# FFN output projection: when weight sums, activation rounding and loads are issued in each step

## The chip, the cores and the metric

One core of one Trainium2 chip runs the kernel. The metric is the device time of one execution in microseconds. Before the change the median of three runs is 2488.52 us (2488.05 to 2489.48).

## The reference

The reference is one layer of a streaming encoder: a normalised mixer (sparse attention and a state-space branch), then a normalised SwiGLU feed-forward network. The change lies in the last matrix product of the network, `f`:

```python
    for _ in range(DEPTH):
        ...
        x = x + gate_m * rmsnorm(mix, post_norm_mix)
        h2 = rmsnorm(x, pre_norm_ffn) * (1.0 + scale_f) + shift_f
        u_gate, u_up = jnp.split(h2 @ w_ffn_in, 2, axis=-1)
        f = (jax.nn.silu(u_gate) * u_up) @ w_ffn_out
        x = x + gate_f * rmsnorm(f, post_norm_ffn)
    return x
```

All arrays are float32. The hidden activation has 1024 positions and 2816 columns, `w_ffn_out` is 2816 by 1024.

## The kernel before

**Tiling.** The product is computed as a Strassen-like scheme of seven half-size products, in the order "1567342". Each of them multiplies a 1408 by 512 combination of weights with a 1408 by 512 combination of activations. The combinations of activations are made earlier (`gate_up`) and lie in device memory (`d_a`). The combinations of weights are made on the way: product 5 sums two blocks into a tile `ws` (L1389), product 6 subtracts from it (L1392), product 7 takes a difference of two fresh blocks (L1395), product 3 uses `ws` again (L1398); products 1, 4 and 2 take a block as it is.

**Precision.** Each float32 operand is split into a rounded part and a rest: ScalarE copies it to the reduced type (`whi`, `ah`, L245), and GpSimd (for weights, `wlo`) or VectorE (for activations, `al`) subtracts (L246). A product of two such pairs takes three matmuls (`P3`: rounded weight with rounded activation, rounded weight with the rest, rest of the weight with rounded activation).

**Steps.** The first six products run as 66 steps, 11 row blocks `j` for each product. A step `i` is 12 matmuls of 128x512 on TensorE (four output blocks `m`, three matmuls each, L1418). While it runs, the step also loads, sums and splits for later steps. Product 2, the seventh, comes last: it is computed in two halves of 256 columns with all 11 row blocks of its weights resident (`late_w`, tiles `wfh` and `wfl`), so that the output can be normalised and written while the second half runs.

**What sets the order.** Inside the block `in_order` (L1457 and on) every engine, and the queue of SyncE that issues all loads, works in exactly the order in which the code is written; nothing overtakes. Engines wait for each other through semaphores alone. A load waits until the tile that it overwrites is free. The buffers that matter are:

- the raw weights (`wraw`): 4 tiles, shared with `gate_up`'s weights;
- the rounded weights and their rests (`whi`, `wlo`): 3 tiles each, so the weights for step `i + 2` can be written once step `i - 1` has been multiplied;
- `EV`: 9 tiles for raw activations (`al`, as loaded), the second block of product 7 (`wt`) and sums of squares;
- `H_` (32) and `Q` (26): the split activations of one product each in turn, the `ws` tiles and the resident weights.

A name can stand for two tiles: `al` is a raw activation as loaded and also the rest that is made from it.

In a step before the change VectorE and ScalarE first make the weights of step `i + 2` (sum, then `whi`), and then the activations of the next product (`ah`, then `al`); between them VectorE or ScalarE takes the result of the product that has ended out of PSUM (`evict`, four times for each product). In product 4's steps the block also loads and splits one row block of the resident weights for each step.

Of the kernel before, what the change touches and what calls it, by code (L numbers as in the profile page):

```python
# [11 lines left out]
F32R = mybir.dt.float32r  # L12
BF = mybir.dt.bfloat16
AF = mybir.ActivationFunctionType
OP = mybir.AluOpType
# [25 lines left out]
PRODUCT = {n: i for i, n in enumerate("1567342")}  # L41
# [26 lines left out]
def build(tc, a, dbg=None, stop=99, slots=None):  # L68
# [9 lines left out]
    H_ = Arena(ctx, tc, "H", n_slots["H"], 512)  # L78
# [13 lines left out]
    def f(x):  # L92
        return x.bitcast(F32)
# [39 lines left out]
    class Stream:  # L133
# [13 lines left out]
        def load(self):  # L147
            src, kt = self.q[len(self.tiles)]
            raw, hi, lo = self.tile(0, F32), self.tile(1, F32R), self.tile(2, F32R)
            behind(SP.dma_start(raw[:, :kt], src))  # L150
            behind(S.activation(hi[:, :kt], raw[:, :kt], AF.Copy))  # L151
            behind(G.tensor_tensor(lo[:, :kt], raw[:, :kt], f(hi[:, :kt]), op=OP.subtract))  # L152
            self.tiles.append((hi, lo))
# [90 lines left out]
    def split_to(src, hi, lo, lo_eng=None):  # L244
        S.activation(hi, src, AF.Copy)  # L245
        (lo_eng or V).tensor_tensor(lo, src, f(hi), op=OP.subtract)  # L246

    def split(alloc, src, name, shape=None, lo_eng=None):
        hi = alloc(name + "h", shape, F32R)
        lo = alloc(name + "l", shape, F32R)  # L250
        split_to(src, hi, lo, lo_eng)
        return hi, lo
# [14 lines left out]
    def rspread(r, nt=4):  # L267
        pt = bank("prn")
        for t in range(nt):
            T.transpose(pt[:, t * P:(t + 1) * P], r[:, t:t + 1].to_broadcast([P, P]), ident)  # L270
        return pt
# [1093 lines left out]
    def flat(t):  # L1365
        return t.rearrange("p m n -> p (m n)")
# [4 lines left out]
    def out_load(name, j):  # L1371

        def load(k, m, to=None):
            r = flat(W.tile(0, F32)) if to is None else to
            SP.dma_start(r, a["w_ffn_out"][k][:, 512 * m:512 * m + 512])
            return r

        k1, k2 = 2 * j, 2 * j + 1
        if name == "5":
            S_[j] = load(k1, 1, place(j)("ws"))  # L1380
            return load(k2, 1)
        if name == "7":
            return load(k1, 0), load(k1, 1, EV("wt"))
        return load(*{"1": (k1, 0), "6": (k1, 0), "3": (k2, 0), "4": (k2, 1), "2": (k2, 0)}[name])

    def out_weights(name, j, raw, alloc=None, lo_eng=G):
        if name == "5":
            w = S_[j]
            V.tensor_tensor(w, w, raw, op=OP.add)  # L1389
        elif name == "6":  # L1390
            w = S_[j]
            V.tensor_tensor(w, w, raw, op=OP.subtract)  # L1392
        elif name == "7":
            w = raw[0]
            V.tensor_tensor(w, w, raw[1], op=OP.subtract)  # L1395
        elif name == "3":
            w = S_.pop(j)
            V.tensor_tensor(w, raw, w, op=OP.subtract)  # L1398
        else:
            w = raw  # L1400
        if alloc is None:
            hi, lo = (flat(W.tile(x, F32R)) for x in (1, 2))
        else:
            hi, lo = alloc("wfh", dt=F32R), alloc("wfl", dt=F32R)
        split_to(w, hi, lo, lo_eng=lo_eng)
        return hi, lo

    def act_load(name, j):
        r = EV("al")
        SP.dma_start(r, d_a[PRODUCT[name], j])  # L1410
        return r

    def act_split(name, r):
        return split((H_, Q)[PRODUCT[name] % 2], r, "a")

    def out_mm(o, w, x, m, cl, j):
        for k, (wi, xi) in enumerate(P3):
            T.matmul(o, w[wi][:, P * m:P * m + P], x[xi][:, cl], start=j == 0 and k == 0, stop=j == NP - 1 and k == 2)  # L1418

    def quarter(m):  # L1420
        return [y[:, half(b)] for y in (acc_[m], acc_[4 + m]) for b in BS]
# [14 lines left out]
    def squared(y, cn, sacc):  # L1436
        sq = EV("sqm")[:, 0:cn]
        S.activation(sq, y, AF.Square)
        if sacc is not None:
            V.tensor_tensor(sq, sq, sacc, op=OP.add)  # L1440
        return sq
# [15 lines left out]
    with in_order(mybir.EngineType.PE, mybir.EngineType.Activation, mybir.EngineType.DVE,  # L1457
                  mybir.EngineType.Pool, mybir.EngineType.SP):
        steps = [(n, j) for n in ORDER[:-1] for j in range(NP)]
        raws, ws, xs, late_w = {}, {}, {}, []  # L1460

        def raw_ahead(i):
            if i < len(steps):
                raws[steps[i]] = out_load(*steps[i])

        def weights_ahead(i):
            if i < len(steps):
                ws[steps[i]] = out_weights(*steps[i], raws.pop(steps[i]))

        raw_ahead(0)  # L1470
        raw_ahead(1)
        for j in range(NP):
            xs["1", j] = act_split("1", act_load("1", j))
            if j < 2:
                weights_ahead(j)
                raw_ahead(j + 2)
        before, banks, s1, prf = None, None, None, None
        for i, (name, j) in enumerate(steps):
            n = ORDER.index(name)
            nxt = ORDER[n + 1]  # L1480
            r = act_load(nxt, j)
            raw_ahead(i + 4)
            late = out_load("2", j) if name == "4" else None
            if j == 0:
                if banks:
                    before = steps[i - 1][0], banks
                banks = [(bank_d if n % 2 and m < 3 else bank)("pfo") for m in range(4)]
            x, w = xs.pop((name, j)), ws.pop((name, j))
            for m in range(4):
                out_mm(banks[m], w, x, m, ALL, j)  # L1490
            if before and j < 4:
                evict(before[0], j, before[1][j])
            weights_ahead(i + 2)
            xs[nxt, j] = act_split(nxt, r)
            if late is not None:
                late_w.append(out_weights("2", j, late, H_ if j < 5 else Q, G if j % 2 else V))
            if name == "3" and 1 <= j < 9:
                c11, c12, c21, c22 = quarter((j - 1) // 2)
                if j % 2:
                    V.tensor_tensor(c12, c12, c22, op=OP.add)  # L1500
                else:
                    V.tensor_tensor(c22, c22, c21, op=OP.add)
                    s1 = squared(c22, 512, s1)
            if name == "4":
                if 1 <= j < 5:
                    s1 = squared(quarter(j - 1)[1], 512, s1)
                if j == 7:
                    r1 = rstd([s1], D)
                if j == 9:
                    prf = rspread(r1)  # L1510
        last, s0, before = banks, None, None
        x1_load(512, 512, 0, 1, 2, 3)
        for c in BS:
            cl, sacc = slice(256 * c, 256 * c + 256), None
            for m in range(4):
                p = bank("pfl")[:, 0:256]
                for j in range(NP):
                    out_mm(p, late_w[j], xs["2", j], m, cl, j)
                if c == 0:
                    evict("4", m, last[m])  # L1520
                    s0 = squared(quarter(m)[2], 512, s0)
                    if m < 2:
                        x1_load(512, 512, 2 * m + 4, 2 * m + 5)
                    else:
                        x1_load(0, 256, 2 * m - 4, 2 * m - 3)
                elif m < 2:
                    x1_load(0, 256, 2 * m + 4, 2 * m + 5)
                V.tensor_tensor(acc_[m][:, cl], acc_[m][:, cl], p, op=OP.add)
                sacc = squared(acc_[m][:, cl], 256, s0[:, 256:512] if c and m == 0 else sacc)
                if c == 0:  # L1530
                    output(2 * m, 512, 512, prf, False)
                    output(2 * m + 1, 512, 512, prf, False)
                elif m == 0:
                    r0 = rstd([before, s0[:, 0:256]], D, nt=2)
                elif m == 1:
                    prf = rspread(r0, 2)
                if c and m > 0:
                    for t in ((0, 1, 2, 3), (4, 5, 6, 7), ())[m - 1]:
                        output(t, 0, 256, prf, False)
                    x1_load(256, 256, *((0, 1, 2, 3), (4, 5, 6, 7), ())[m - 1])  # L1540
            before = sacc
        prf = rspread(rstd([before], D, nt=2), 2)
        for t in range(8):
            output(t, 256, 256, prf, True)
# [78 lines left out]
```

## Time and profile before

| what | value |
|---|---|
| median of three runs | 2488.52 us |
| the profiled execution's own time | 2489.43 us |
| span of the profile, first to last instruction | 2487.6 us |
| TensorE busy | 2377.9 us, 96% of the span |
| VectorE, ScalarE, GpSimd busy | 1599.2, 1245.6, 1036.2 us |
| mean granted TensorE clock | 0.987 |
| the steps of the six products | from 2213.4 to about 2441.25 us |

A row of a timeline gives the start and the duration in us, the engine (PE is TensorE, DVE is VectorE, ACT is ScalarE, POOL is GpSimd, SPq is the queue of SyncE that issues loads), the line of the kernel, the operation and its tiles, and in brackets how long the engine sat idle before it and on whom it waited. A row of the stretches gives the time from and to, its length, and for each engine the busy time with the number of instructions. Matmuls overlap each other, so a busy time of TensorE close to the length does not mean that it runs at its best rate; the distance between the first matmuls of two steps does.

### The profile page before, as it was taken

Reading aid. Unit: us, or ns where it says so; the run is one execution under the profiler, and the core shown is the slowest. Engines: PE = TensorE matmul, PEld = TensorE weight load, DVE = VectorE, ACT = ScalarE, POOL = GpSimd, SP = SyncE. Lnnn points to the kernel's source line nnn. Section 1 sums busy time; section 2 is a strip of 40 time slices with the busy share of each in tenths; the row PEclk is TensorE's granted clock in tenths of the full one; section 3 lists DMA queues with packets and bytes.
Section 4 is the critical chain, followed back from the end, with each engine's and each line's share of the span. In section 5 each row is a group of like instructions: output and inputs, shape, how many; then the busy total and the mean of one; then the engine's idle time right before and its main releaser. Section 6 shows DMA issues by size and latency. Waiting matters only on the chain. (4 is left out here: it accounts for less than half of the span.)

```text
span 2487.6 us, 35107 instructions
## 1 busy us (share of the span) xinstructions
PE 2377.9 (96%) x11878; PEld 1910.2 (77%) x11878; DVE 1599.2 (64%) x3115; ACT 1245.6 (50%) x2350; POOL 1036.2 (42%) x848
## 2 busy tenths in 40 slices
PE   7999999999899999999999999998999999999887
PEld 5888888887678787777776777877877888877656
DVE  4467775798855667765557685445376877456665
ACT  3456665567365664455666565533443223344342
POOL 1321112222443335422335346566576555544334
PEclk9999999999999999999999999999999999999999
DMA  7123123423322334213669885654555555256645
GB/s 265 62 88 123 64 68 95 144 93 112 104 90 87 98 98 132 77 35 107 216 217 301 262 246 170 203 174 128 177 189 172 182 177 170 93 193 209 203 136 186
DMA packets 227652, 369.85 MB, mean 149 GB/s; under 512 B 22624, under 2 KB 84752, under 8 KB 227472
## 3 DMA queue, kind: packets, MB, share of 16 engines
q1 hardware_dynamic: 226752, 367.03, 45.8%
q8 instruction: 94, 1.54, 0.3%
q14 instruction: 86, 0.70, 0.1%
q10 hardware_dynamic: 720, 0.58, 0.1%
HBM read 275.74 MB, written 94.92 MB: 149 GB/s over the span
## 5 line engine op out<-in xcount | busy, mean ns | idle before, releaser
L152 POOL TENSOR_TENSOR wlo<-wraw,whi 128x512 fp32r<-128x512 f32 x242 | 330.0, 1366 | 596.7 <-ACT whi L151 540.0
L1254 PE MATMUL p<-xh,wr 128*128 128x512 f32 x880 | 276.3, 392 | 5.9 <-DVE g L1304 4.3
L151 ACT ACTIVATE whi<-wraw 128x512 fp32r<-128x512 f32 x242 | 151.7, 629 | 229.7 <-issue 67.4
L1248 POOL TENSOR_TENSOR wr<-a,wr 128x512 fp32r<-128x512 f32 x110 | 156.9, 1434 | 124.7 <-ACT wr L1247 99.5
L1254 PEld LDWEIGHTS p<-xh,wr 128*128 128x128 f32 x880 | 166.4, 189 | 41.9 <-DVE g L1304 4.7
L1254 PE MATMUL p<-xl,wr 128*128 128x512 f32 x440 | 172.2, 391 | 0.0
L778 ACT ACTIVATE lg<-lg,mx 128x256 f32<-128x256 f32 (+7 forms) x128 | 98.7, 773 | 95.2 <-DVE mx L775 93.1
L246 DVE TENSOR_TENSOR al<-al,ah 128x512 fp32r<-128x512 f32 x77 | 92.5, 1207 | 78.6 <-ACT ah L245 78.2
L1247 ACT ACTIVATE wr<-a 128x512 fp32r<-128x512 f32 x110 | 68.6, 631 | 143.0 <-PE p L1254 116.7
L1418 PE MATMUL pfo<-ah,wlo 128*128 128x512 f32 x264 | 108.9, 412 | 20.0 <-POOL wlo L246 19.9
L1254 PE MATMUL p<-h2h,wr 128*128 128x512 f32 x352 | 111.9, 394 | 0.0
L1418 PE MATMUL pfo<-ah,whi 128*128 128x512 f32 x264 | 105.7, 400 | 3.9 <-ACT whi L245 3.6
L638 ACT ACTIVATE junk<-acc,cand__2182 128x1024 bf16<-128x1024 f32 (+2 forms) x96 | 86.4, 900 | 45.7 <-DVE cand__2182 L681 28.7
L225 PE MATMUL pos<-yh,wlo 128*128 128x512 f32 x256 | 101.1, 396 | 2.7 <-POOL wlo L152 2.7
L1418 PE MATMUL pfo<-al,whi 128*128 128x512 f32 x264 | 103.6, 392 | 0.0
L225 PE MATMUL pos<-yh,whi 128*128 128x512 f32 x256 | 100.9, 395 | 2.4 <-ACT yh L1120 1.4
L589 DVE SCALAR_TENSOR_TENSOR acc<-rel,widx,acc 128x384 f32<-128x384 f32 (+2 forms) x90 | 87.1, 988 | 24.7 <-ACT rel L584 24.5
L799 PE MATMUL pt<-ident,lg 128*128 128x128 f32 x576 | 90.1, 279 | 12.4 <-ACT lg L778 11.2
L584 ACT ACTIVATE rel<-prel 128x512 f32<-128x512 f32 (+3 forms) x160 | 77.3, 524 | 48.0 <-PE prel L583 44.4
L225 PE MATMUL pos<-yw,whi 128*128 128x512 f32 x256 | 100.3, 392 | 0.0
L1254 PEld LDWEIGHTS p<-xl,wr 128*128 128x128 f32 x440 | 83.2, 189 | 17.3
L904 DVE SCALAR_TENSOR_TENSOR cv<-pw,vec,cv 128x511 f32<-128x511 f32 (+2 forms) x96 | 71.3, 743 | 34.6 <-ACT cv L901 34.5
(580 smaller groups left out, 7189.4 us busy)
## 6 DMA issues: line engine op xcount, KB each, us to landing
wraw<-w_in SPq DMA_DIRECT2D x130, 256.0 KB, 2.9
a<-w_ffn_in SPq DMA_DIRECT2D x120, 256.0 KB, 3.3
wraw<-w_ffn_out SPq DMA_DIRECT2D x77, 256.0 KB, 3.1
al<-d_a SPq DMA_DIRECT2D x77, 256.0 KB, 3.6
adaw<-ada_w SPq DMA_DIRECT2D x64, 256.0 KB, 3.0
al<-d_ac SPq DMA_DIRECT2D x32, 512.0 KB, 5.4
wraw<-w_o_ssd SPq DMA_DIRECT2D x64, 256.0 KB, 3.0
d_a<-kept SPq DMA_DIRECT2D x33, 256.0 KB, 3.3
```

The source lines that it names most:

```text
L151: behind(S.activation(hi[:, :kt], raw[:, :kt], AF.Copy))
L152: behind(G.tensor_tensor(lo[:, :kt], raw[:, :kt], f(hi[:, :kt]), op=OP.subtract))
L225: T.matmul(o, wt[:, k0 + i, :], xs[k][xi][b][:, sl], start=pi == 0 and i == 0 and wt is hi and xi == 0, stop=pi == len(pcs) - 1 and i == l ...
L246: (lo_eng or V).tensor_tensor(lo, src, f(hi), op=OP.subtract)
L584: S.activation(rel[:, 512 * b:512 * b + w_], pr[:, 0:w_], AF.Relu)
L589: V.scalar_tensor_tensor(acc[i][:, 0:n], rel[:, 0:n], ws, acc[i][:, 0:n], op0=OP.mult, op1=OP.add)
L638: S.activation(jk, y, AF.Sign, scale=-1.0, bias=a_, accum_out=o)
L778: S.activation(lg[:, 0:n], lg[:, 0:n], AF.Exp, scale=-1.0, bias=m, accum_out=mx[:, 3:4])
L799: T.transpose(ptv[:, hh, t, :], PR[hh, t][:, j * P:(j + 1) * P], ident)
L1248: G.tensor_tensor(w[:, 1], src, f(w[:, 0]), op=OP.subtract)
L1254: T.matmul(p, w[:, wi, i], X[x][i][xi], start=start and i == 0 and k == 0, stop=i == 3 and k == 2, skip_group_check=True)
L1418: T.matmul(o, w[wi][:, P * m:P * m + P], x[xi][:, cl], start=j == 0 and k == 0, stop=j == NP - 1 and k == 2)
```

## The change

Inside the 66 steps four things move.

1. The sum of the weights is a function of its own (`out_sum`) and is made for step `i + 3`, ahead of everything else that the step does on VectorE. Rounding and splitting the weights (`out_weights`) stays at step `i + 2`.
2. ScalarE rounds the activations (`ah`) first in a step, and `whi` after it. The raw activations are loaded one step earlier (`al_ahead(i + 1)`). VectorE's `al` now comes behind the eviction.
3. Raw weights are loaded five steps ahead where it was four; four of them are issued ahead of the first activations.
4. The resident weights of product 2 are loaded into `EV` tiles (`late_load`), not into the raw weights' tiles, two steps ahead of their split, and are spread over steps 48 to 65, that is over products 3 and 4. GpSimd makes all eleven rests; before, VectorE made six of them.

Besides, the sums of squares in product 4 run in its steps 4 to 7 where they ran in 1 to 4, `rstd` stands at its step 8 where it stood at 7, and the spread of its result over the partitions (`rspread`) follows the first group of product 2.

```diff
-    def out_weights(name, j, raw, alloc=None, lo_eng=G):
+    def out_sum(name, j, raw):
         if name == "5":
             w = S_[j]
             V.tensor_tensor(w, w, raw, op=OP.add)
...
         else:
             w = raw
-        if alloc is None:
-            hi, lo = (flat(W.tile(x, F32R)) for x in (1, 2))
-        else:
-            hi, lo = alloc("wfh", dt=F32R), alloc("wfl", dt=F32R)
-        split_to(w, hi, lo, lo_eng=lo_eng)
+        return w
+
+    def out_weights(w):
+        hi, lo = (flat(W.tile(x, F32R)) for x in (1, 2))
+        split_to(w, hi, lo, lo_eng=G)
         return hi, lo
+
+    def late_load(j):
+        r = EV("late")
+        SP.dma_start(r, a["w_ffn_out"][2 * j + 1][:, 0:512])
+        return r
+
+    def late_split(j, r):
+        return split(H_ if j < 5 else Q, r, "wf", lo_eng=G)
...
-        raws, ws, xs, late_w = {}, {}, {}, []
+        late_at = {4 * NP + 4 + (5 * j + 1) // 3: j for j in range(NP)}
+        raws, ws, xs, als, late_r, late_w = {}, {}, {}, {}, {}, []
...
-        raw_ahead(0)
-        raw_ahead(1)
+        for i in range(4):
+            raw_ahead(i)
         for j in range(NP):
-            xs["1", j] = act_split("1", act_load("1", j))
+            r = act_load("1", j)
             if j < 2:
-                weights_ahead(j)
-                raw_ahead(j + 2)
-        before, banks, s1, prf = None, None, None, None
+                ws[j] = out_weights(raws.pop(j))
+            xs["1", j] = act_split("1", r)
+        raw_ahead(4)
+        al_ahead(0)
...
-            r = act_load(nxt, j)
-            raw_ahead(i + 4)
-            late = out_load("2", j) if name == "4" else None
+            al_ahead(i + 1)
+            raw_ahead(i + 5)
+            if i + 2 in late_at:
+                late_r[i + 2] = late_load(late_at[i + 2])
...
             for m in range(4):
                 out_mm(banks[m], w, x, m, ALL, j)
+            sum_ahead(i + 3)
+            r = als.pop(i)
+            hi, lo = (alloc("a" + k, None, F32R) for k in "hl" for alloc in [(H_, Q)[PRODUCT[nxt] % 2]])
+            S.activation(hi, r, AF.Copy)
+            if i + 2 < len(steps):
+                ws[i + 2] = out_weights(raws.pop(i + 2))
             if before and j < 4:
                 evict(before[0], j, before[1][j])
-            weights_ahead(i + 2)
-            xs[nxt, j] = act_split(nxt, r)
-            if late is not None:
-                late_w.append(out_weights("2", j, late, H_ if j < 5 else Q, G if j % 2 else V))
+            V.tensor_tensor(lo, r, f(hi), op=OP.subtract)
+            xs[nxt, j] = hi, lo
+            if i in late_at:
+                late_w.append(late_split(late_at[i], late_r.pop(i)))
...
             if name == "4":
-                if 1 <= j < 5:
-                    s1 = squared(quarter(j - 1)[1], 512, s1)
-                if j == 7:
+                if 4 <= j < 8:
+                    s1 = squared(quarter(j - 4)[1], 512, s1)
+                if j == 8:
                     r1 = rstd([s1], D)
-                if j == 9:
-                    prf = rspread(r1)
...
+                if c == m == 0:
+                    prf = rspread(r1)
```

**Sums and rounding, in the middle of the steps.** These are ScalarE's instructions around the end of product 6, before the change. The numbers tell the tiles apart; VectorE's sum for `ws_20759` and its rest from `ah_21130` stand beside each other in VectorE's own order.

```order
L245 ACTIVATE whi_21101<-ws_20733 128x512
L245 ACTIVATE ah_21105<-al_21084 128x512
L245 ACTIVATE whi_21126<-ws_20759 128x512
L245 ACTIVATE ah_21130<-al_21109 128x512
L1426 ACTIVATE acc4_20473<-pfo_20843 128x512
```

```order
L1392 TENSOR_TENSOR ws_20733<-ws_20733,wraw_21036 128x512
L246 TENSOR_TENSOR al_21106<-al_21084,ah_21105 128x512
L1392 TENSOR_TENSOR ws_20759<-ws_20759,wraw_21061 128x512
L246 TENSOR_TENSOR al_21131<-al_21109,ah_21130 128x512
L1392 TENSOR_TENSOR ws_20785<-ws_20785,wraw_21086 128x512
```

The same place after the change, ScalarE and then VectorE:

```order
L1510 ACTIVATE ah_21106<-al_21064 128x512
L245 ACTIVATE whi_21109<-ws_20713 128x512
L1510 ACTIVATE ah_21131<-al_21089 128x512
L245 ACTIVATE whi_21134<-ws_20739 128x512
L1510 ACTIVATE ah_21160<-al_21114 128x512
```

```order
L1392 TENSOR_TENSOR ws_20739<-ws_20739,wraw_21041 128x512
L1515 TENSOR_TENSOR al_21107<-al_21064,ah_21106 128x512
L1392 TENSOR_TENSOR ws_20765<-ws_20765,wraw_21066 128x512
L1515 TENSOR_TENSOR al_21132<-al_21089,ah_21131 128x512
L1392 TENSOR_TENSOR ws_20792<-ws_20792,wraw_21091 128x512
```

Before, the rounding `whi_21126` needs the sum `ws_20759` that VectorE does just ahead of it, `ah_21130` stands behind that rounding on ScalarE, and VectorE's `al_21131` needs `ah_21130`; the next sum stands behind `al_21131`. After the change `ah_21106` stands ahead of the rounding, and the rounding behind it (`whi_21109`) takes the sum of the step before (`ws_20713`).

**Loads at the start.** The queue of SyncE around the first steps; lines with a minus stand there before, lines with a plus after the change. L1375 loads raw weights, L1410 (L1418 after) raw activations, and L1324 to L1342 write `gate_up`'s results.

```order
 L1324 DMA d_a<-g_20108 128x512
+L1375 DMA wraw<-w_ffn_out 128x512
 L1326 DMA d_a<-kept 128x512
 L1328 DMA d_a<-kept 128x512
+L1375 DMA wraw<-w_ffn_out 128x512
 L1340 DMA d_a<-p_20069 128x512
 L1342 DMA d_a<-u_20126 128x512
 L1336 DMA d_a<-p_20212 128x512
 L1338 DMA d_a<-kept 128x512
-L1410 DMA al<-d_a 128x512
-L1375 DMA wraw<-w_ffn_out 128x512
-L1410 DMA al<-d_a 128x512
```

The third and fourth raw weights are issued ahead of `gate_up`'s stores and of the first activations.

**Rests of the resident weights.** GpSimd's order in products 3 and 4, before the change:

```order
L246 TENSOR_TENSOR wlo<-ws,whi 128x512 x11
L246 TENSOR_TENSOR wlo<-wraw,whi 128x512 x4
L246 TENSOR_TENSOR wfl<-wraw,wfh 128x512
L246 TENSOR_TENSOR wlo<-wraw,whi 128x512 x2
L246 TENSOR_TENSOR wfl<-wraw,wfh 128x512
```

and after it:

```order
L246 TENSOR_TENSOR wlo<-ws,whi 128x512 x7
L246 TENSOR_TENSOR wfl<-late,wfh 128x512
L246 TENSOR_TENSOR wlo<-ws,whi 128x512 x2
L246 TENSOR_TENSOR wfl<-late,wfh 128x512
L246 TENSOR_TENSOR wlo<-ws,whi 128x512
L246 TENSOR_TENSOR wfl<-late,wfh 128x512
```

GpSimd's first resident rest comes eight weights earlier, in product 3, and there are eleven of them where there were five.

More of the change, by code (lines that the diff above doesn't have):

```diff
@@ L1383, in out_load @@
             return load(k1, 0), load(k1, 1, EV("wt"))
-        return load(*{"1": (k1, 0), "6": (k1, 0), "3": (k2, 0), "4": (k2, 1), "2": (k2, 0)}[name])
-    def out_weights(name, j, raw, alloc=None, lo_eng=G):
+        return load(*{"1": (k1, 0), "6": (k1, 0), "3": (k2, 0), "4": (k2, 1)}[name])
+    def out_sum(name, j, raw):
         if name == "5":
@@ L1459, in build, with sum_ahead, al_ahead @@
         steps = [(n, j) for n in ORDER[:-1] for j in range(NP)]
-        raws, ws, xs, late_w = {}, {}, {}, []
+        late_at = {4 * NP + 4 + (5 * j + 1) // 3: j for j in range(NP)}
+        raws, ws, xs, als, late_r, late_w = {}, {}, {}, {}, {}, []
         def raw_ahead(i):
             if i < len(steps):
-                raws[steps[i]] = out_load(*steps[i])
-        def weights_ahead(i):
+                raws[i] = out_load(*steps[i])
+        def sum_ahead(i):
             if i < len(steps):
-                ws[steps[i]] = out_weights(*steps[i], raws.pop(steps[i]))
-        raw_ahead(0)
-        raw_ahead(1)
+                raws[i] = out_sum(*steps[i], raws[i])
+        def al_ahead(i):
+            if i < len(steps):
+                als[i] = act_load(ORDER[i // NP + 1], steps[i][1])
+        for i in range(4):
+            raw_ahead(i)
         for j in range(NP):
-            xs["1", j] = act_split("1", act_load("1", j))
+            r = act_load("1", j)
             if j < 2:
-                weights_ahead(j)
-                raw_ahead(j + 2)
-        before, banks, s1, prf = None, None, None, None
+                ws[j] = out_weights(raws.pop(j))
+            xs["1", j] = act_split("1", r)
+        raw_ahead(4)
+        al_ahead(0)
+        before, banks, s1 = None, None, None
         for i, (name, j) in enumerate(steps):
@@ L1487, in build @@
                 banks = [(bank_d if n % 2 and m < 3 else bank)("pfo") for m in range(4)]
-            x, w = xs.pop((name, j)), ws.pop((name, j))
+            x, w = xs.pop((name, j)), ws.pop(i)
             for m in range(4):
                 out_mm(banks[m], w, x, m, ALL, j)
+            sum_ahead(i + 3)
[4 more added lines that the diff above has]
+                ws[i + 2] = out_weights(raws.pop(i + 2))
             if before and j < 4:
                 evict(before[0], j, before[1][j])
-            weights_ahead(i + 2)
-            xs[nxt, j] = act_split(nxt, r)
-            if late is not None:
-                late_w.append(out_weights("2", j, late, H_ if j < 5 else Q, G if j % 2 else V))
+            V.tensor_tensor(lo, r, f(hi), op=OP.subtract)
+            xs[nxt, j] = hi, lo
+            if i in late_at:
+                late_w.append(late_split(late_at[i], late_r.pop(i)))
             if name == "3" and 1 <= j < 9:
```

## The prediction

> **What bounds the kernel now.** I read the page's groups first, then the stretches of the six products, then TensorE's timeline inside them, and the waits last. The stage from 2213.4 to 2441.25 us is the one that the change touches. Its busy rows, for the matmuls of the steps and the evictions alone:
>
> ```profile
> 2213.40:2248.10 34.70, 30.68 (x133) 24.63 (x133) 0.00 (x0) 0.55 (x1) 1.00 0.91 294
> 2248.10:2280.40 32.30, 31.33 (x134) 24.41 (x133) 0.00 (x0) 1.77 (x4) 1.00 0.68 215
> 2280.40:2316.30 35.90, 33.16 (x134) 23.89 (x132) 0.00 (x0) 2.32 (x4) 1.00 0.62 190
> 2316.30:2354.50 38.20, 33.95 (x133) 23.61 (x132) 2.70 (x4) 0.00 (x0) 1.00 0.61 197
> 2354.50:2400.10 45.60, 36.49 (x133) 24.53 (x133) 2.70 (x4) 0.00 (x0) 0.96 0.38 129
> 2400.10:2441.25 41.15, 33.56 (x133) 23.59 (x131) 2.71 (x4) 0.00 (x0) 1.00 0.61 194
> ```
>
> The stretches are products 1, 5, 6, 7, 3 and 4, each from its first matmul to the next product's first (132 matmuls; a row counts one or two over the edge). After the length come TensorE, weight loads, VectorE, ScalarE, then clock, DMA share and GB/s. The same work takes 32.3 to 45.6 us, so something other than TensorE sets it. What TensorE can do is seen where it waits for nothing, at the first matmuls of steps 6 and 7:
>
> ```profile
> 2234.48 0.39 PE L1418 MATMUL pfo<-ah,whi 128*128 128x512 f32 x1
> 2237.20 0.39 PE L1418 MATMUL pfo<-ah,whi 128*128 128x512 f32 x1
> ```
>
> A step at TensorE's rate is 2.72 us, a product 11 x 2.72 = 29.92 us. Product 1's stretch also holds 12 matmuls of `gate_up`, so it could take 32.64. Against that the products lose 2.1, 2.4, 6.0, 8.3, 15.7 and 11.2 us: **45.7 us** in all, all that can be won here. The page says whom TensorE waits for:
>
> ```profile
> L1418 PE MATMUL pfo<-ah,wlo 128*128 128x512 f32 x264 | 108.9, 412 | 20.0 <-POOL wlo L246 19.9
> ```
>
> It is the weights' rest, GpSimd's last link. But GpSimd is not full; its own wait leads back through ScalarE to VectorE. One turn in product 6, in order of time:
>
> ```profile
> 2294.71 0.68 DVE L1392 TENSOR_TENSOR ws<-ws,wraw 128x512 f32<-128x512 f32 x1
> 2295.50 0.63 ACT L245 ACTIVATE whi<-ws 128x512 fp32r<-128x512 f32 x1 [1.62 <-DVE ws L1392]
> 2296.04 0.62 ACT L245 ACTIVATE ah<-al 128x512 fp32r<-128x512 f32 x1
> 2296.22 1.29 POOL L246 TENSOR_TENSOR wlo<-ws,whi 128x512 fp32r<-128x512 f32 x1 [1.97 <-ACT whi L245]
> 2296.69 1.36 DVE L246 TENSOR_TENSOR al<-al,ah 128x512 fp32r<-128x512 f32 x1 [1.30 <-ACT ah L245]
> 2297.97 0.68 DVE L1392 TENSOR_TENSOR ws<-ws,wraw 128x512 f32<-128x512 f32 x1
> ```
>
> This is a **ring**: sum, rounding of the weight, rounding of the activation behind it, the activation's rest, and only then the next sum. Its turn is 2297.97 - 2294.71 = 3.26 us, more than 2.72, so it sets the pace. The `al` takes 1.36 us, not 0.69, since it starts in the middle of GpSimd's `wlo` and ends 0.54 us after that (2297.51 to 2298.05): the two do not run at once. Two more rows show both halves of this:
>
> ```profile
> 2400.93 3.44 POOL L246 TENSOR_TENSOR wlo<-wraw,whi 128x512 fp32r<-128x512 f32 x2
> 2401.44 1.78 DVE L246 TENSOR_TENSOR al<-al,ah 128x512 fp32r<-128x512 f32 x1
> 2403.14 0.67 DVE L1432 TENSOR_TENSOR acc<-acc,pfo 128x512 f32<-128x512 f32 x1
> 2403.74 1.18 DVE L246 TENSOR_TENSOR al<-al,ah 128x512 fp32r<-128x512 f32 x1
> ```
>
> Around GpSimd's work up to 2404.37, two `al` are stretched, while the eviction between them, which reads PSUM, keeps its 0.67 us. So only operations with both inputs in SBUF share something with GpSimd. In product 3 the ring holds still more:
>
> ```profile
> 2379.54 0.68 DVE L1502 TENSOR_TENSOR acc<-acc 128x512 f32<-128x512 f32 x1
> 2380.92 0.69 DVE L1440 TENSOR_TENSOR sqm<-sqm 128x512 f32<-128x512 f32 x1 [0.70 <-ACT sqm L1438]
> 2381.53 0.69 DVE L1398 TENSOR_TENSOR ws<-wraw,ws 128x512 f32<-128x512 f32 x1
> ```
>
> The combining of results, and a square that VectorE waits for, stand between `al` and the sum, each 0.6 us or more a turn.
>
> Product 4 has no sums; there ScalarE, and all behind it, wait for the resident weights' load:
>
> ```profile
> ACT wfh L245 <- DMA wraw<-w_ffn_out: 18.8, 9, 3.3
> SPq L1375 <- POOL wlo L246: 11.9, 10, 4.9
> ```
>
> The second row is the load queue, waiting for one of the four raw tiles.
>
> **The change part by part.**
>
> *The sum one step earlier and `ah` first* cut the ring. The rounding then uses a sum of the step before, and `ah` depends on nothing made in this step. What limits a step now is each engine's own work: ScalarE two roundings of about 0.54 from start to start (2295.50 to 2296.04), 1.1 us; VectorE two operations at 0.6 (2380.92 to 2381.53), 1.2, plus 0.6 where it evicts; and what VectorE and GpSimd may not do at once, 1.29 + 0.6 + 0.6 = 2.49 us. All are under 2.72. So products 5, 6 and 7 should run at TensorE's rate: 2.4 + 6.0 + 8.3 = 16.7 us removed. In the four evicting steps of product 7, if evictions did count, 3.09 us stand against 2.72; the seven other steps win back 7 x 0.23 = 1.6, as much as the 4 x 0.37 = 1.5 lost. I leave 1 us for the three products: **15.7 gained**, bounds 10 (the tail of a late load in each) and 16.7.
>
> *The resident weights.* Their loads leave the raw tiles for `EV`, so product 4's wait on `wraw` goes; what replaces it is work. For the shared part I add, at 1.29 for GpSimd and 0.6 for VectorE: product 3 has 11 `wlo` and 4 resident rests (19.4), 11 `al`, 8 sums, 8 combinings and 3 additions of squares (30 x 0.6 = 18.0), in all 37.4 against 29.9. Product 4 has 9 `wlo` and 7 resident rests (20.6), 11 `al` and 4 additions (9.0): 29.6 against 29.9. Product 3 thus falls 7.5 us behind, and step by step the lag still grows to about 10 at steps 61 to 63, where a resident rest, a square, an `al` and a `wlo` come together (3.8 us a step), before the last `wlo` are done and it shrinks. Not all of a lag reaches TensorE: product 5 before lost only 2.4 us though 11 turns at 3.26 are 5.9 over the rate, so the pairs of weights made ahead cover 3.5. I take 10 - 3.5 = 6.5, with 0.5 for `rstd` of the squares, whose last square stands one step ahead of it where it stood three: **7 us lost** of the 26.9 that products 3 and 4 lose now, 19.9 gained. Bounds: 3, if late work of VectorE need not be done in time (activations' rests are wanted a product later), and 13, if evictions cannot use the gaps either (8 x 0.6) and the 1.45 us `pow` of GpSimd is on the path.
>
> The row that speaks against part of this is the price of the six rests that move from VectorE to GpSimd:
>
> ```profile
> L246 DVE TENSOR_TENSOR wfl<-wraw,wfh 128x512 fp32r<-128x512 f32 x6 | 4.7, 785 | 7.6 <-ACT wfh L245 7.6
> L246 POOL TENSOR_TENSOR wfl<-wraw,wfh 128x512 fp32r<-128x512 f32 x5 | 6.8, 1351 | 7.2 <-ACT wfh L245 7.2
> ```
>
> Six times 1.29 for 0.6 is 4.1 us more of the shared time, and it is in the 37.4 and 29.6 above. The Trainium skill, "Perfetto Trace Analysis", section "Optimizing Scalar/DVE Operations", warns that VectorE and GpSimd share a read port of SBUF, so that moving work between the two might not help. By that rule alone this edit would give nothing back; the trace agrees with the port (the stretched `al`), and the sum already holds the loss.
>
> *The start.* Product 1's loss is one stall:
>
> ```profile
> 2206.35 9.51 SPq L1410 DMA_DIRECT2D al<-d_a  x8
> 2220.61 0.64 ACT L245 ACTIVATE ah<-al 128x512 fp32r<-128x512 f32 x1 [1.74 <-DMA al<-d_a]
> 2221.15 0.62 ACT L245 ACTIVATE whi<-wraw 128x512 fp32r<-128x512 f32 x1
> 2221.85 2.02 POOL L246 TENSOR_TENSOR wlo<-wraw,whi 128x512 fp32r<-128x512 f32 x1 [9.39 <-ACT whi L245]
> ```
>
> The third step's rounding stands behind eleven `ah`, and their loads wait for `EV` tiles (9.51 us for eight). After the change one more `ah` stands ahead of that rounding, but the first weight's is done before and two raw loads have left the queue's way: 0.4 + 0.5 us sooner for the loads, 0.5 later for the extra `ah`. The first `al` are also less in GpSimd's way. I take a loss of 1 instead of 2.1: **1.1 gained**, bounds -2.7 (a whole step later, if the extra `ah` waits for a load that is issued after the eleventh) and 2.1.
>
> *Loads five ahead* cost no engine time. Each load of a step without a sum waits for the `wlo` one step nearer than before, so the distance from free tile to use stays four steps. The `rspread` is four transposes of TensorE at either place; I count its move as nothing.
>
> **Sum:** 15.7 + 19.9 + 1.1 = 36.7 us. The profiled execution took 2489.43 (span 2487.6 and 1.83 around it), 0.9 above the median of the runs. 2489.4 - 36.7 = 2452.7; its counterpart as a median is 2451.8. I say **2453**, a little up since the unknowns mostly add stalls.
>
> **The rivals.**
>
> *The shared time takes the ring's place everywhere* (VectorE blocked in its order by GpSimd, so that evictions wait too). For it: the 2.49 of 2.72 leaves 0.23 a step. Against it: 0.67 for an eviction inside GpSimd's work. Products 5 to 7 then lose 4 and products 3 and 4 the upper 13, the start 1: 18 us remain, 27.7 gained, **2461**.
>
> *Loads take its place.* Chain: `wlo` frees a raw tile, the queue issues weights and activations (0.4 + 0.4), the load lands, then `ah`, `whi`, `wlo` (0.5, 0.7, 1.3), three steps ahead of use: a step is a third of the landing time + 3.3. Landing times in the busiest stretch, 2220 to 2262 us:
>
> ```profile
> al<-d_a SPq DMA_DIRECT2D x17, 256.0 KB, 4.3
> wraw<-w_ffn_out SPq DMA_DIRECT2D x16, 256.0 KB, 3.9
> d_a<-u SPq DMA_DIRECT2D x1, 256.0 KB, 5.6
> ```
>
> At 4.3 a step is 2.5, hidden; from 4.9 on it shows. At 5.6 it is 2.97: 0.25 over 33 steps (products 1, 7 and 4) is 8 more than my remaining 9, so 28.7 gained, **2460**. Products 5 and 7 ask for 768 KB in 2.72 us, 289 GB/s, close to the 294 of the first stretch, where DMA was 0.91 busy.
>
> *Slower.* The same chain with `ah` ahead of `whi`: if faster steps push the landing to 10 us, a step is 4.4, 1.7 over in 33 steps = 56, with the 9 that remain 65 against 45.7: about 19 slower, **2508**. It decides against the change from a landing of about 8.2 us on; nothing in the trace is above 5.6.
>
> *The change does not do what it says:* the ring closes over another link (a tile that both sides wait for), the step stays at 3.26 and the time at **2488**. The two orders show no such link.
>
> **How the numbers follow.** Forecast 0.70 (2444 to 2457), shared time 0.12, loads 0.08, another ring 0.04, slower 0.06. The floor is 2488.5 - 45.7, about 2443. The range takes in the bounds of products 3 and 4 and of the start and most of both milder rivals: 2445 to 2471. About 0.2% is what a measurement of this kernel can tell from no change. Faster 0.91, same 0.03, slower 0.06.
>
> **What would show it.** In products 5, 6 and 7 the first matmuls of steps should stand 2.72 us apart and ScalarE's `whi` should wait for TensorE (a free tile), not for VectorE's sum. In product 4 the wait on the load of resident weights should be gone. Products 3 and 4 together should take 62 to 73 us where they took 86.75. Wrong would be: steps of 3 us or more in product 6, `ah` waiting for DMA in most steps, or TensorE waiting long at `rstd`.

## The result, and the profile after

The changed kernel takes 2450.26 us (median of four runs, 2449.83 to 2451.43) against 2488.82 us of the kernel before, run beside it: a ratio of 0.9846, 95% interval 0.9829 to 0.9863, or 38.6 us less. The prediction said 2453 us.

The stretches of products 1, 5, 6, 7, 3 and 4 after the change, columns as in the prediction (from and to, length, busy time and number of instructions of TensorE, weight loads, VectorE and ScalarE, clock, DMA share, GB/s):

```profile
2213.33:2247.05 33.72, 30.54 (x132) 24.63 (x132) 0.00 (x0) 0.00 (x0) 1.00 0.87 285
2247.05:2276.97 29.92, 29.92 (x133) 24.78 (x132) 0.00 (x0) 2.32 (x4) 1.00 0.90 309
2276.97:2306.89 29.92, 29.92 (x133) 24.78 (x132) 0.69 (x1) 2.32 (x4) 1.00 0.60 191
2306.89:2336.81 29.92, 29.92 (x133) 24.78 (x132) 2.73 (x4) 0.00 (x0) 1.00 0.87 289
2336.81:2367.99 31.18, 30.46 (x134) 24.44 (x132) 2.02 (x3) 0.00 (x0) 1.00 0.53 173
2367.99:2401.48 33.49, 30.91 (x132) 24.46 (x132) 3.39 (x5) 0.00 (x0) 1.00 0.69 229
```

Products 5, 6 and 7 now take 29.92 us, which is 11 steps at TensorE's rate of 2.72. The six stretches sum to 188.15 us where they took 227.97 with the same boundaries (first matmul of the steps to the first of product 2): 39.8 us less. From there to the end it is 46.6 us, and was 46.2. All of the gain lies in the stage that was changed. TensorE's wait for the weights' rest, 20.0 us on the page before, is nearly gone:

```profile
L1426 PE MATMUL pfo<-ah,wlo 128*128 128x512 f32 x264 | 103.2, 391 | 2.1 <-POOL wlo L246 2.1
```

One step of product 6, in order of time:

```profile
2290.35 0.68 DVE L1392 TENSOR_TENSOR ws<-ws,wraw 128x512 f32<-128x512 f32 x1
2290.59 0.63 ACT L245 ACTIVATE whi<-ws 128x512 fp32r<-128x512 f32 x1 [1.57 <-POOL wlo L246]
2291.13 0.61 ACT L1510 ACTIVATE ah<-al 128x512 fp32r<-128x512 f32 x1
2291.30 1.29 POOL L246 TENSOR_TENSOR wlo<-ws,whi 128x512 fp32r<-128x512 f32 x1 [1.43 <-ACT whi L245]
2291.78 1.37 DVE L1515 TENSOR_TENSOR al<-al,ah 128x512 fp32r<-128x512 f32 x1 [0.75 <-ACT ah L1510]
2293.07 0.68 DVE L1392 TENSOR_TENSOR ws<-ws,wraw 128x512 f32<-128x512 f32 x1
```

The rounding `whi` at 2290.59 starts while the sum at 2290.35 still runs, so it uses an earlier sum. It starts at the first matmul of its step (2290.57); what held it is the weight tile that TensorE gives back there. The row names GpSimd, whose `wlo` had ended 0.7 us before: a wait for several engines is put down to one. `al` still takes 1.37 us in GpSimd's shadow, but from one sum to the next it is 2293.07 - 2290.35 = 2.72 us.

What is left in the stage above 2.72 us a step is 1.0 us at step 2, 3.1 in steps 53 to 56, and 1.65 at step 63.

### The profile page after: what moved, and what is told of

Read it like the earlier page. It is cut to its first block, busy times and chain, and to the rows that moved or that the text cites. A ratio compares the mean times of both kernels' runs of the same rounds, so it can differ in the third digit from the quotient of the medians.

```text
span 2448.1 us, 35113 instructions
## 1 busy us (share of the span) xinstructions
PE 2360.6 (96%) x11878; PEld 1915.1 (78%) x11878; DVE 1598.2 (65%) x3109; ACT 1242.6 (51%) x2350; POOL 1052.2 (43%) x854
## 5 line engine op out<-in xcount | busy, mean ns | idle before, releaser
L1426 PE MATMUL pfo<-ah,wlo 128*128 128x512 f32 x264 | 103.2, 391 | 2.1 <-POOL wlo L246 2.1
L1515 DVE TENSOR_TENSOR al<-al,ah 128x512 fp32r<-128x512 f32 x66 | 74.6, 1132 | 33.0 <-ACT ah L1510 32.7
```

The costliest lines, as they stand in the source:

```text
L1515: V.tensor_tensor(lo, r, f(hi), op=OP.subtract)
```

## The experiments

All are edits of the changed kernel. The stage's length (first matmul of the steps to product 2) is compared across runs, since the part of the kernel ahead of it differs by several us from execution to execution (it ends between 2208.3 and 2217.6 us in the profiles of this document). Each stage is that of one profiled execution; the changed kernel has 188.15 and, run again, 188.56. The ratio is to the kernel before on the same chip.

### Which half of the order cuts the ring

First, ScalarE makes the weight's rounding ahead of the activation's again; the sum stays a step early.

```diff
-            S.activation(hi, r, AF.Copy)
             if i + 2 < len(steps):
                 ws[i + 2] = out_weights(raws.pop(i + 2))
+            S.activation(hi, r, AF.Copy)
```

> One half of the ring's cut is undone: ScalarE makes the weight's rounding first again and the activation's rounding behind it; the sum stays one step early. Ring theory (either half alone cuts the ring, since the rounding then uses a sum of the step before): products 5, 6 and 7 stay at 2.72 us a step, 2450 to 2453 us. Rival A (the rounding of activations first is what matters): the step goes back to about 3.26, products 5 to 7 lose some 16 us and product 3 more, 2466 to 2480. Rival B (the loads further ahead bring the gain, the order nothing): 2450.

Ratio 0.9848 (0.9834 to 0.9863), median 2454.2 us. Products 5 to 7 take 29.92 us each, stage 190.87. Product 1 loses nothing here, but products 3 and 4 take 68.5 us, 3.8 more than in the changed kernel: the place of the activation's rounding counts there, though not for the ring. Then the other half: the sum for step `i + 2` again, the activation's rounding still first.

```diff
-            sum_ahead(i + 3)
+            sum_ahead(i + 2)
```

> The other half is undone: the sum is made for step i + 2 again, ahead of its rounding in the same step; the activation's rounding stays first. Ring theory: the activation's rest no longer waits for the weight's rounding, so no ring; 2.72 us a step in products 5 to 7, 2450 to 2456 us (some cushion is lost in product 3, where the sum stands behind VectorE's lag). Rival A' (the early sum is what matters): 3.26 a step, 2466 to 2480. Rival B (loads): 2450.

Ratio 0.9832 (0.9816 to 0.9849), 2451.26 us; products 5 to 7 at 29.92 again, stage 189.09. Then both undone, with the eviction ahead as it was; all loads and the resident weights stay as changed.

```diff
-            sum_ahead(i + 3)
...
-            S.activation(hi, r, AF.Copy)
-            if i + 2 < len(steps):
-                ws[i + 2] = out_weights(raws.pop(i + 2))
             if before and j < 4:
                 evict(before[0], j, before[1][j])
+            sum_ahead(i + 2)
+            if i + 2 < len(steps):
+                ws[i + 2] = out_weights(raws.pop(i + 2))
+            r = als.pop(i)
...
+            S.activation(hi, r, AF.Copy)
```

> Both halves are undone: eviction, sum for i + 2, weight's rounding, activation's rounding, activation's rest, in the order of the kernel before; the loads five and one ahead and the spread resident weights stay as changed. Ring theory: steps of 3.26 us in products 5 to 7 and of 3.85 and more in product 3 return; some 16 us there, 12 or more in product 3; 2478 to 2486 us. Rival B (loads bring the gain): 2450 to 2453.

Ratio 0.9975 (0.9962 to 0.9988), 2483.67 us. Products 5, 6, 7 and 3 of this kernel:

```profile
2241.31:2273.55 32.24, 31.22 (x133) 24.39 (x132) 0.00 (x0) 1.78 (x4) 1.00 0.65 215
2273.55:2309.48 35.93, 33.13 (x133) 23.92 (x132) 0.00 (x0) 2.32 (x4) 1.00 0.60 190
2309.48:2347.74 38.26, 34.03 (x133) 23.62 (x132) 2.70 (x4) 0.00 (x0) 1.00 0.58 196
2347.74:2396.52 48.78, 37.45 (x134) 25.39 (x132) 2.70 (x4) 0.00 (x0) 0.93 0.44 148
```

32.24, 35.93 and 38.26 us are, within 0.04, the 32.28, 35.94 and 38.24 of the kernel before. The ring is the cause of what products 5 to 7 lost, either half alone opens it, and the loads alone leave it closed. Products 3 and 4 take 84.7 us together here, 2.2 less than before the change: the new tiles and the spread bring little without the new order.

### The resident weights

They go back to product 4's steps, to the raw weights' tiles, and to both engines; the order of the steps stays as changed.

```diff
-        r = EV("late")
+        r = flat(W.tile(0, F32))
...
-        return split(H_ if j < 5 else Q, r, "wf", lo_eng=G)
+        return split(H_ if j < 5 else Q, r, "wf", lo_eng=G if j % 2 else V)
...
-            if i + 2 in late_at:
-                late_r[i + 2] = late_load(late_at[i + 2])
+            if name == "4":
+                late_r[i] = late_load(j)
...
-            if i in late_at:
-                late_w.append(late_split(late_at[i], late_r.pop(i)))
+            if name == "4":
+                late_w.append(late_split(j, late_r.pop(i)))
```

> The resident weights go back: loaded into the raw weights' tiles in product 4's steps, one a step, rests by VectorE and GpSimd in turn; the order of the steps stays as changed. If their loads' tiles are what costs product 4 its time: product 3 at 30 us, product 4 back towards 41, in all +5 to +9, 2455 to 2459 us. Rival (the ring in the steps was the cause there too, the loads hidden): 2449 to 2451.

Ratio 0.9915 (0.9899 to 0.9932), 2470.19 us: the direction was right, the size not. Product 3 runs at 29.92, product 4 takes 54.45 us, more than the 41.15 before the change:

```profile
2365.89:2420.34 54.45, 39.68 (x133) 28.01 (x131) 3.08 (x5) 0.00 (x0) 0.87 0.49 159
```

The wait for the resident weights' load is back and longer (before: 18.8 us, nine times):

```profile
ACT wfh L245 <- DMA wraw<-w_ffn_out: 32.4, 10, 5.8
```

Products 3 and 4 take 84.4 us together: the new order without the new tiles and the spread brings 2.5 of the 22.2 us that the two bring together. Why product 4 is worse than before shows in its middle (L1410 is the resident weights' load here):

```profile
2379.86 1.71 POOL L246 TENSOR_TENSOR wlo<-wraw,whi 128x512 fp32r<-128x512 f32 x1
2381.59 0.33 SPq L1410 DMA_DIRECT2D wraw<-w_ffn_out  x1
2384.31 0.63 ACT L245 ACTIVATE wfh<-wraw 128x512 fp32r<-128x512 f32 x1 [4.71 <-DMA wraw<-w_ffn_out]
2385.36 0.61 ACT L245 ACTIVATE whi<-wraw 128x512 fp32r<-128x512 f32 x1
2386.05 1.27 POOL L246 TENSOR_TENSOR wlo<-wraw,whi 128x512 fp32r<-128x512 f32 x1 [4.49 <-ACT whi L245]
2387.35 0.33 SPq L1410 DMA_DIRECT2D wraw<-w_ffn_out  x1
```

A resident load starts only when a `wlo` has ended (2379.86 + 1.71 = 2381.57) and freed a tile. ScalarE stands until it lands, the next `whi` and `wlo` stand behind, and the next resident load behind that `wlo`: another ring, with a turn of 2387.35 - 2381.59 = 5.76 us. That the raw loads, now five ahead, close it by taking all four tiles is argued; a kernel with the old tiles and loads four ahead was not run.

Then only the rests: VectorE makes every second one again.

```diff
-        return split(H_ if j < 5 else Q, r, "wf", lo_eng=G)
+        return split(H_ if j < 5 else Q, r, "wf", lo_eng=G if j % 2 else V)
```

> VectorE makes every second rest of the resident weights again, as before the change; loads and spread stay as changed. By the shared time (1.29 us on GpSimd against 0.6 on VectorE) this frees some 4 us in products 3 and 4: 2446 to 2449 us. Rival (in a full stretch VectorE and GpSimd take turns one by one, 1.7 us a pair, and VectorE's own queue is the late one, with the squares behind it): no gain or a loss, 2450 to 2454.

Ratio 0.9844 (0.9831 to 0.9858), 2448.91 us, stage 189.21, products 3 and 4 at 31.43 and 33.63. No gain: the 4 us of shared time that this frees were not what TensorE waited for.

### What stalls products 3 and 4

The changed kernel's profile shows the stall ahead of step 55, in order of time:

```profile
2361.59 1.74 POOL L246 TENSOR_TENSOR wfl<-late,wfh 128x512 fp32r<-128x512 f32 x1
2362.10 1.78 DVE L1522 TENSOR_TENSOR acc<-acc,acc 128x512 f32<-128x512 f32 x1
2363.29 1.72 POOL L246 TENSOR_TENSOR wlo<-ws,whi 128x512 fp32r<-128x512 f32 x1
2363.80 1.76 DVE L1515 TENSOR_TENSOR al<-al,ah 128x512 fp32r<-128x512 f32 x1
2365.49 0.68 DVE L1524 TENSOR_TENSOR acc<-acc 128x512 f32<-128x512 f32 x1
2366.26 0.63 ACT L1446 ACTIVATE sqm<-acc 128x512 f32<-128x512 f32 x1 [4.51 <-DVE acc L1524]
2366.80 0.62 ACT L1510 ACTIVATE ah<-al 128x512 fp32r<-128x512 f32 x1
2367.32 0.61 ACT L245 ACTIVATE whi<-wraw 128x512 fp32r<-128x512 f32 x1
2367.99 0.50 PE L1426 MATMUL pfo<-ah,whi 128*128 128x512 f32 x1 [0.36 <-ACT whi L245]
```

VectorE and GpSimd take turns, one operation each, about 1.70 us a pair. VectorE is behind, and ScalarE stands for 4.51 us at the square of a result that VectorE has yet to combine (L1524). The rounding that TensorE needs stands behind that square. The other stall is `rstd` at step 63:

```profile
2395.00 1.05 PE L259 MATMUL p<-ones,sqm 128*128 128x1 f32 x8 [0.58 <-DVE sqm L1448]
```

So the squares of product 3 were moved to product 4's first four steps, and `rstd` to its last; the same work in all.

```diff
                     V.tensor_tensor(c22, c22, c21, op=OP.add)
-                    s1 = squared(c22, 512, s1)
             if name == "4":
-                if 4 <= j < 8:
-                    s1 = squared(quarter(j - 4)[1], 512, s1)
-                if j == 8:
+                if j < 8:
+                    s1 = squared(quarter(j % 4)[1 if j > 3 else 3], 512, s1)
+                if j == 10:
                     r1 = rstd([s1], D)
```

> The squares of product 3's combined results move to the first four steps of product 4 and rstd of the sum to product 4's last step; nothing else. Theory 1 (TensorE's stalls at steps 53 to 56 come from ScalarE standing at a square until VectorE has combined, with the roundings behind it, and the one at step 63 from rstd one step behind its last square): about 3 and 1.7 us go, 2445 to 2447 us. Theory 2 (VectorE's and GpSimd's shared time is too short in products 3 and 4, as the prediction summed it, so the stall only moves): within 1.5 us of 2450.

Ratio 0.9826 (0.9813 to 0.984), 2446.41 us, stage 185.02: product 3 at 29.92 and product 4 at 30.73, in which the only longer step is the last (3.53 us, with `rstd`'s matmuls). The squares also take three additions of VectorE out of product 3, but VectorE is nearly as late as before:

```profile
2369.69 1.78 DVE L1524 TENSOR_TENSOR acc<-acc 128x512 f32<-128x512 f32 x1
```

This last combining starts 27.7 us after product 3's first matmul (2341.97), where it started after 28.7 (2365.49 and 2336.81). It ends at 2371.47, and product 4's first matmul comes 0.42 us later without a wait (2371.89). In the changed kernel that matmul comes 1.8 us after the combining's end (2366.17 to 2367.99), with the square and two roundings between. So it is the square's place that stalled TensorE. `rstd` alone moved:

```diff
-                if j == 8:
+                if j == 10:
                     r1 = rstd([s1], D)
```

> Only rstd moves, from product 4's step 8 to its last step. Theory 1: the stall of 1.65 us at step 63 goes, 2448 to 2449 us. Theory 2: the lag that it showed comes out later, 2450.

Ratio 0.9831 (0.9818 to 0.9845), 2445.86 us, but the stage is 188.35: step 63 is at 2.72, steps 64 and 65 take 3.28 and 3.53. 0.81 us are the matmuls themselves wherever they stand; the rest of the stall moved on. The two ratios overlap; the stages tell the kernels apart: the squares are worth 3.3 us (3.6 in products 3 and 4 alone), `rstd`'s place nearly nothing without them, against the 1.7 that was expected.

### What VectorE and GpSimd share

In products 5 to 7 VectorE makes each activation's rest twice.

```diff
             V.tensor_tensor(lo, r, f(hi), op=OP.subtract)
+            if NP <= i < 4 * NP:
+                V.tensor_tensor(lo, r, f(hi), op=OP.subtract)
```

> In the steps of products 5, 6 and 7 VectorE makes each activation's rest twice, the same subtraction again. If operations with both inputs in SBUF share one thing with GpSimd, a step holds 1.29 + 3 x 0.6 = 3.09 us of it against TensorE's 2.72, so of 33 x 0.37 = 12 us about 8 show after the cushion: 2456 to 2460 us; with 1.7 us a pair of turns instead of 1.89 it is 2.9 a step, some 3 us, 2452 to 2455. Rival (VectorE's own time is what counts, 1.8 of 2.72 us, 2.4 where it evicts): within 1 us of 2450.

Ratio 0.9906 (0.9893 to 0.992), 2465.34 us, stage 208.66. That is more than the 2460 expected. Steps stay at 2.72 up to step 29; then most of those of product 7 take about 3.0 us:

```profile
2296.46 1.78 DVE L1392 TENSOR_TENSOR ws<-ws,wraw 128x512 f32<-128x512 f32 x1
2298.16 0.68 DVE L1515 TENSOR_TENSOR al<-al,ah 128x512 fp32r<-128x512 f32 x1
2298.87 0.69 DVE L1517 TENSOR_TENSOR al<-al,ah 128x512 fp32r<-128x512 f32 x1
2299.06 1.66 POOL L246 TENSOR_TENSOR wlo<-ws,whi 128x512 fp32r<-128x512 f32 x1 [1.37 <-ACT whi L245]
2299.48 1.78 DVE L1392 TENSOR_TENSOR ws<-ws,wraw 128x512 f32<-128x512 f32 x1
```

A turn is 2299.48 - 2296.46 = 3.02 us, between the 2.9 and the 3.09 of the two sums in the expectation. VectorE has no pause in it. The lag before it shows, 19 steps (11 to 29) by 0.31, is estimated from this at 5.9 us. Steps 37 to 40, behind VectorE's evictions in product 7, take 3.46 to 3.61 us: where VectorE itself is full, an eviction costs its own time. Products 5 to 7 lose 6.0 us, and products 3 and 4 another 12.1 against the changed kernel's second run (76.53 and 64.44), since VectorE comes to them late. The remaining 2 of the stage's 20 us lie at the start, ahead of the first step that was edited. Its counterpart is an operation of the same size with one input in PSUM:

```diff
+            if NP <= i < 4 * NP and j < 9:
+                V.tensor_tensor(lo, r, before[1][j % 4], op=OP.subtract)
             V.tensor_tensor(lo, r, f(hi), op=OP.subtract)
```

> In the first nine steps of products 5, 6 and 7 VectorE does one more subtraction of 512 columns, with one input in PSUM (the result of the product before) and one in SBUF; its output is overwritten by the activation's rest. Beside it stands the kernel with one more subtraction whose inputs are both in SBUF, which lost 20 us. If only two SBUF inputs share with GpSimd: VectorE's own 1.8 of 2.72 us (2.4 where it evicts) is enough and the stage stays within 1.5 us of 188 (up to 190). Rival (any operation of VectorE counts): steps of 3.0 us again, 27 of 33 extra ones, stage 200 or more.

Ratio 0.9848 (0.9827 to 0.9869), 2449.46 us, stage 189.26, products 5 to 7 at 29.92. The extra operation (L1516) is not stretched by GpSimd's (all 27 take 0.67 to 0.69 us, some of them wholly inside GpSimd's), the next one (L1517) is:

```profile
2294.36 0.67 DVE L1516 TENSOR_TENSOR al<-al,pfo 128x512 fp32r<-128x512 f32 x1
2294.70 1.30 POOL L246 TENSOR_TENSOR wlo<-ws,whi 128x512 fp32r<-128x512 f32 x1 [1.42 <-ACT whi L245]
2295.13 1.42 DVE L1517 TENSOR_TENSOR al<-al,ah 128x512 fp32r<-128x512 f32 x1
```

The Trainium skill, "SBUF — State Buffer", section "Who interferes with whom", says that a VectorE instruction with two SBUF inputs contends with a GpSimd instruction that reads SBUF, and one with at most one SBUF input outside its two-port modes does not. Both kernels agree: about 18 us for the one, 0.7 for the other.

### Loads, start, and all together

On one chip: the changed kernel again, raw loads four steps ahead, and a kernel with the squares and `rstd` moved and, in the first four steps, the weight's rounding first.

> The changed kernel itself, so that the next three can be compared with it on one chip. Stage from the first matmul of the steps to product 2 near 188 us, as before; ratio near 0.985.

Ratio 0.9838 (0.982 to 0.9856), 2448.93 us, stage 188.56.

```diff
-        raw_ahead(4)
         al_ahead(0)
...
-            raw_ahead(i + 5)
+            raw_ahead(i + 4)
```

> Raw weights are loaded four steps ahead again, three issued... four ahead of the first activations stay; all else as changed. Prediction's claim: five ahead is worth nothing by itself, stage 188 to 189 us, within 1 us of the changed kernel. Rival (a sum made three steps ahead has one step less for its load, so with four ahead VectorE waits for the load in each step of products 5 to 3, with the rest behind it): 3 us or more lost, stage 191 to 200.

Ratio 0.983 (0.9812 to 0.9847), 2447.75 us, stage 187.03: loads five ahead bring nothing.

```diff
+            if i < 4:
+                ws[i + 2] = out_weights(raws.pop(i + 2))
             r = als.pop(i)
...
             S.activation(hi, r, AF.Copy)
-            if i + 2 < len(steps):
+            if 4 <= i < len(steps) - 2:
                 ws[i + 2] = out_weights(raws.pop(i + 2))
...
```

The lines left out at the end are those of the squares and `rstd` above.

> The squares and rstd later, and in the first four steps the weight's rounding ahead of the activation's. The two kernels with that rounding ahead in all steps lost nothing in product 1, those with it behind lost 1 to 2.1 us at steps 1 and 2. If the order there is the cause: no loss at the start, 0.8 at rstd, stage 183 us, 5 us less than the changed kernel run beside it, ratio to it 0.998. Rival (the start is set by when the activations' loads land, and differs from run to run): stage 184 to 185.

Ratio 0.9808 (0.979 to 0.9826), 2441.98 us, about 7 less than the changed kernel beside it. The stage is 183.29, 5.3 less; the rest lies outside it. Its first and its last two stretches:

```profile
2212.75:2245.63 32.88, 30.32 (x133) 24.70 (x132) 0.00 (x0) 0.00 (x0) 1.00 0.85 292
...
2335.39:2365.31 29.92, 29.92 (x134) 24.77 (x132) 2.02 (x3) 0.00 (x0) 1.00 0.62 210
2365.31:2396.04 30.73, 30.08 (x133) 24.59 (x131) 2.70 (x4) 0.00 (x0) 1.00 0.71 232
```

At the start 0.24 us is lost; both kernels with that rounding ahead in every step lost none, those with it behind 0.8 to 2.1 (the kernel with the rests made twice 3.8).

## Why the prediction was right, point by point

**The ring** carried the forecast, and it held: 15.7 us were counted for products 5 to 7, 16.7 came (106.46 to 89.76 us). The 1 us kept back for late loads was not needed. The prediction named the two edits together; either alone does it.

**Products 3 and 4**: 19.9 us gained and 7 still lost were forecast; 22.2 were gained (86.86 to 64.67) and 4.8 are lost, 0.8 of that being `rstd`'s own matmuls. The size was near, the reason not. The step that failed is "10 - 3.5 = 6.5", the shared time less a cushion. Moving four squares removes nearly all of the loss with the same work on VectorE and GpSimd and VectorE nearly as late, so the shared time was enough. The cushion of 3.5 was taken from a kernel without the early sum (an estimated 5.9 us in the kernel with two rests), and a pair in turn costs 1.70, not the 1.89 that was added up. What the sum left out is ScalarE: a square that waits for VectorE's lag holds the rounding behind it.

**The price of the moved rests**, 4.1 us of shared time, was in the sum. The run with the rests on both engines shows no gain from paying less (stage 189.21 against 188.15 and 188.56). That fits the warning of the Trainium skill, "Perfetto Trace Analysis", section "Optimizing Scalar/DVE Operations", which the prediction took up: moving work between the two might not help.

**The start**: 1.1 forecast, 0.9 gained in this profile, 0.3 in the second one (34.36). The number was near partly by luck, since two of its terms were too small and nearly cancel:

```profile
2218.18 0.63 ACT L245 ACTIVATE ah<-al 128x512 fp32r<-128x512 f32 x1 [1.01 <-DMA al<-d_a]
2220.33 0.63 ACT L1510 ACTIVATE ah<-al 128x512 fp32r<-128x512 f32 x1 [1.52 <-DMA al<-d_a]
2220.87 0.61 ACT L245 ACTIVATE whi<-wraw 128x512 fp32r<-128x512 f32 x1
```

The eleventh `ah` starts at 2218.18, 2.4 us sooner than before (2220.61), where 0.9 was counted. But the extra `ah` behind it waits 1.52 us for a load that was issued later, the case that the prediction kept for its lower bound. So the third step's rounding starts 2.15 us after 2218.72 (2218.18 + 0.54), where it could have followed the eleventh `ah`; 0.5 was counted. It comes only 0.28 us sooner than before (2221.15). The other 0.7 is GpSimd's rest of that weight, which took 2.02 us before and takes 1.28 here, as the prediction had it without a number.

**Loads five ahead** at nothing: right. **The rivals**: an operation that reads PSUM is not held by GpSimd (the PSUM run), and products 5 to 7 run at TensorE's rate, so the shared time did not take the ring's place. The loads did get slower, past the 4.9 us from which the prediction let them show (the same window, 2220 to 2262 us):

```profile
wraw<-w_ffn_out SPq DMA_DIRECT2D x18, 256.0 KB, 5.1
al<-d_a SPq DMA_DIRECT2D x18, 256.0 KB, 5.3
```

`ah` waits for its load in nine of product 7's eleven steps (7.3 us in all) and in most of products 1 and 4, which the prediction had named as a sign of being wrong. Yet from step 3 on every step of products 1, 5, 6 and 7 is 2.72 us, so the sign was too strict. By the rival's own chain 5.3 us is 0.15 us a step, 1.2 over product 1's last eight steps, less than the cushion. The slower case asked for 8.2.

The median is 2.7 us below the forecast. Of that, 1.2 is what the forecast stood above its own sum (2451.8). The stage gained 39.8 where 36.7 were counted: 1.0 more in products 5 to 7, 2.3 more in products 3 and 4, 0.2 less at the start. Another 0.4 was lost behind the stage, and the rest is within the spread of the runs (2449.83 to 2451.43).

## What to carry to other kernels

When TensorE waits for one engine's last link and no engine is full, follow the waits until they come back to where they began: the length of that ring, not any engine's load, is the period, and taking one dependency out of the step opened it here. Once it is open, look in each in-order queue for an instruction that waits for a late engine (here a square) and move it behind the work that is due. An engine's total time says little about such stalls.

## What was not expected of the hardware

VectorE and GpSimd under full load take turns one for one: in product 3 of the changed kernel GpSimd's 1.29 us operations become 1.71 to 1.74 and VectorE's 0.69 us ones 1.76 to 1.79, a pair every 1.70 us. That is less than the 1.29 + 0.6 of the two in a row.

With the old place of the resident weights and the new order, product 4 takes 54.45 us, longer than either kernel: the new order and the new tiles were not independent. In products 3 and 4 each alone brings some 2 us, both together 22. Why the changed kernel loses 1.1 us at the start in one profile and 1.7 in another is open.
